# Attention projections as seven block products over two units at a time

## The chip, the core and the metric

The kernel runs on one core of one Trainium2 chip. Five engines work side by side, each through its own instructions in their order: TensorE (PE, matmuls and transposes), VectorE (DVE), ScalarE (ACT), GpSimd (POOL) and SyncE (SP, which issues every DMA of this kernel). They meet at semaphores. Operands lie in SBUF, matmuls write to PSUM, inputs, outputs and spilled tiles lie in DRAM. The metric is the device time of one execution in microseconds, lower is better.

## What is computed

The reference is a trunk of two layers over a sequence of 1024 positions and a width of 1024. Layer 0 mixes tokens with dilated sliding-window attention, layer 1 with a gated linear recurrence; each mixer is followed by a LayerNorm, a squared-ReLU MLP and another LayerNorm. The change is in the first mixer:

```python
def dilated_attention_mixer(x, w_in, w_out):
    B, S, _ = x.shape
    proj = (x @ w_in).reshape(B, S, N_GROUPS, 3, ATTN_HEADS, ATTN_HEAD_DIM)
    pos = jnp.arange(S)
    outs, lses = [], []
    for g, (window, dilation) in enumerate(DILATED_PATTERNS):
        q = rotary(proj[:, :, g, 0], pos)
        k = rotary(proj[:, :, g, 1], pos)
        o, lse = dilated_window_attention(q, k, proj[:, :, g, 2], window, dilation)
        outs.append(o)
        lses.append(lse)
    wts = jax.nn.softmax(jnp.stack(lses, axis=0), axis=0)
    o = jnp.einsum('gbsh,gbshe->bshe', wts, jnp.stack(outs, axis=0).astype(F32))
    return o.reshape(B, S, ATTN_HEADS * ATTN_HEAD_DIM).astype(x.dtype) @ w_out
```

There are 16 heads of 64, three window groups with dilations 1, 4 and 16, and so 9216 projection columns. Results are float32.

## The kernel before

To keep float32 accuracy at the faster matmul type, each operand is split into a high part (a copy rounded by ACT, L98) and a low part (raw minus high, a subtraction on DVE, L99). A product then takes three matmuls: high by high (L132), high weights by low activations (L133), low weights by high activations (L134). The helper `split` records both steps, so L98 and L99 appear for every operand in the kernel.

The unit of attention is a pair of heads in one window group: 8 pairs by 3 groups are 24 units, in the order of dilation 16, 4, 1 within a pair. A unit needs three blocks of 128 projected columns, K, Q and V. x, transposed, lies in SBUF for the whole stage as high and low parts (16 tiles). `prefetch` loads the next weight block of 512 KB and splits it whole, 128x1024. `proj` computes a block for one half of the positions: 8 k blocks by 3 matmuls of 128x512 into one of three PSUM banks ("mm"). ACT copies it out (L529 for Q and K, L533 and L536 for V, which is scattered into the order of the residue classes). When both halves of Q or K are there, `rope` sends four DMAs that swap the halves of the heads into `rot`, multiplies by the cosines on DVE (L344), by the sines on POOL (L345) and adds on DVE (L346).

The attention of a unit is cut into six steps (`pieces`): scores in pairs of blocks (L373), a mask-and-maximum on DVE (L384), exponentials on ACT (L387), transposes of the probabilities (L397, copied out by DVE for odd blocks at L401 and by ACT for even ones at L403), transposes of V (L361, copied by DVE at L362), and PV (L415). A list `fill` hangs these steps behind later half blocks: two half blocks of lag, then one step behind each. Then come `combine_tr` (maxima and sums transposed and sent through DRAM into a layout of 16 rows), `combine` (the weights of the three groups, small DVE operations, L466 to L482, then six pairs of DMAs into `frow`) and `combine_mul` (a matmul that broadcasts the weights, L497, products on DVE, L498 and L500, one addition on POOL, L499). The framework's scheduler may reorder each engine's instructions within what the data allow.

The result of each pair goes to `outproj_ln`: the first five pairs through DRAM (`SPILL`), the rest from SBUF. Its first pass accumulates seven of the eight k blocks for six of the eight row tiles, with what is left in `fill` hung in between; then come the last k block, the residual and the LayerNorm. The MLP's first matmul (L783 to L785) is already computed with seven products of blocks, with its combinations of weights on DVE (L743 to L748) and its sums out of PSUM on DVE (L796 to L818).

All large tiles come from one pool of 45 slots of 128x1024 float32. SP takes DMAs in its order, and one that waits for a slot or a producer holds up those behind it.

## Time and profile before

| what | us |
|---|---|
| median of 3 runs | 3043.63 (3040.58 to 3044.74) |
| the profiled execution | 3044.36 |
| its span, first to last instruction | 3042.6 |
| PE busy in the span | 2928.1 |
| DVE busy | 1904.1 |
| ACT busy | 1336.1 |
| POOL busy | 434.4 |

Busy time of PE is the union of its matmuls, which overlap, so a full PE is not PE at its peak. The granted TensorE clock was 0.986 of full speed over the span. In rows by group a line reads: source line, engine, operation, output from inputs, shapes, count, then busy time in all, mean of one in ns, and the idle time of the engine ahead of it with what ended it. In rows in order of time the first number is the start and the second the duration.

### The profile page before, as it was taken

The numbers are of one execution on the slowest core, as the hardware profiler recorded it, in microseconds if no ns is written. First come the engines' busy times: TensorE is split into PE (matmuls) and PEld (weight loads), VectorE is DVE, ScalarE is ACT, GpSimd is POOL, SyncE is SP. The second block draws the span as 40 slices with busy tenths as digits, with TensorE's granted clock in tenths as the row PEclk, the third lists the DMA queues.
The fourth block names the chain that finished last, engine by engine and source line by source line (L and its number), as shares of the span: only waits on it lengthen the run. The fifth ranks groups of instructions, "written<-read, shape, count | busy, mean of one in ns | idle before, by whom it ended". The sixth has DMA issues, their size and how long they took to land. (4 is left out here: it accounts for less than half of the span.)

```text
span 3042.6 us, 40183 instructions
## 1 busy us (share of the span) xinstructions
PE 2928.1 (96%) x14584; PEld 2325.6 (76%) x14584; DVE 1904.1 (63%) x3432; ACT 1336.1 (44%) x2783; POOL 434.4 (14%) x229
## 2 busy tenths in 40 slices
PE   8999999999999999899999999999999799999998
PEld 6777777777777767677778887787788677778886
DVE  5355555464554466866679786456565866679785
ACT  3343443343343441644454444455561644454442
POOL 1101011110111001200024221101010300025210
PEclk9999999999999999899999999999999899999999
DMA  4222122222222141344465653111132344465662
GB/s 143 63 57 78 44 70 64 58 71 56 60 62 61 54 146 61 124 159 152 140 241 190 212 200 116 44 56 38 54 110 71 121 163 146 141 239 195 208 231 74
DMA packets 166855, 347.78 MB, mean 114 GB/s; under 512 B 26880, under 2 KB 41344, under 8 KB 166656
## 3 DMA queue, kind: packets, MB, share of 16 engines
q1 hardware_dynamic: 166656, 345.21, 35.5%
q8 instruction: 115, 1.88, 0.3%
q14 instruction: 84, 0.69, 0.1%
HBM read 238.43 MB, written 81.13 MB: 105 GB/s over the span
## 5 line engine op out<-in xcount | busy, mean ns | idle before, releaser
L132 PE MATMUL pmm<-xh,wh 128*128 128x512 f32 x1152 | 463.9, 403 | 8.1 <-ACT wh L98 8.1
L134 PE MATMUL pmm<-xh,wl 128*128 128x512 f32 x1152 | 452.5, 393 | 1.7 <-DVE wl L99 1.7
L133 PE MATMUL pmm<-xl,wh 128*128 128x512 f32 x1152 | 453.2, 393 | 0.9 <-DVE xl L99 0.9
L387 ACT ACTIVATE p<-p,stats 128x128 f32<-128x128 f32 (+1 forms) x384 | 168.6, 441 | 227.5 <-DVE stats L384 225.2
L132 PEld LDWEIGHTS pmm<-xh,wh 128*128 128x128 f32 x1152 | 218.1, 189 | 56.7 <-ACT wh L98 8.8
L134 PEld LDWEIGHTS pmm<-xh,wl 128*128 128x128 f32 x1152 | 217.3, 189 | 49.7 <-DVE wl L99 4.0
L133 PEld LDWEIGHTS pmm<-xl,wh 128*128 128x128 f32 x1152 | 217.9, 189 | 43.4 <-DVE xl L99 1.4
L384 DVE CUSTOM_DVE_ANT_0 p<-s,mask 128x128 f32<-128x128 f32 (+1 forms) x384 | 115.5, 348 | 165.5 <-PE s L373 134.3
L345 POOL TENSOR_TENSOR rot<-rot,sinT 128x1024 f32<-128x1024 f32 x48 | 115.3, 2402 | 677.6 <-DMA rot<-e 655.7
L904 PE MATMUL pdy<-dT,dS 128*128 128x512 f32 x512 | 199.4, 389 | 0.7 <-DVE dT L99 0.7
L905 PE MATMUL pdy<-dT,dS 128*128 128x512 f32 x512 | 199.2, 389 | 0.0
L903 PE MATMUL pdy<-dT,dS 128*128 128x512 f32 x512 | 199.2, 389 | 0.0
L98 ACT ACTIVATE dS<-dr 128x512 fp32r<-128x512 f32 x192 | 120.2, 626 | 133.0 <-PE pdy L905 41.0
L99 DVE TENSOR_TENSOR dS<-dr,dS 128x512 fp32r<-128x512 f32 x192 | 165.6, 862 | 11.6 <-ACT dS L98 11.2
L99 DVE TENSOR_TENSOR wl<-wr,wh 128x1024 fp32r<-128x1024 f32 (+1 forms) x97 | 126.5, 1305 | 55.6 <-ACT wh L98 54.8
L132 PE MATMUL pmm<-f0nh,wh 128*128 128x512 f32 x384 | 153.5, 400 | 0.8 <-ACT wh L98 0.8
L133 PE MATMUL pmm<-f0nl,wh 128*128 128x512 f32 x384 | 150.0, 391 | 0.0
L134 PE MATMUL pmm<-f0nh,wl 128*128 128x512 f32 x384 | 149.9, 390 | 0.0
L529 ACT ACTIVATE e<-pmm 128x512 f32<-128x512 f32 x96 | 55.9, 590 | 207.1 <-PE pmm L134 204.6
L98 ACT ACTIVATE wh<-wr 128x1024 fp32r<-128x1024 f32 (+1 forms) x97 | 101.0, 1041 | 87.1 <-DMA wr<-in_w_attn_dram 59.0
L875 POOL TENSOR_TENSOR hold<-hold,dr 128x512 f32<-128x512 f32 x32 | 48.3, 1510 | 631.5 <-PE pup L785 599.3
L99 DVE TENSOR_TENSOR dT<-dr,dT 128x512 fp32r<-128x512 f32 x128 | 121.8, 963 | 7.5 <-ACT dT L98 6.6
(370 smaller groups left out, 6856.6 us busy)
## 6 DMA issues: line engine op xcount, KB each, us to landing
...
dr<-in_w_down_dram SPq DMA_DIRECT2D x160, 256.0 KB
...
```

The lines of the kernel that those rows point to most:

```text
L98: act(hi, raw, AF.Copy)
L99: nc.vector.tensor_sub(lo, raw, hi.bitcast(F32))
L132: nc.tensor.matmul(o, wh[:, k], xs.h(k), start=k == 0, stop=False)
L133: nc.tensor.matmul(o, wh[:, k], xs.l(k), start=False, stop=False)
L134: nc.tensor.matmul(o, wl[:, k], xs.h(k), start=False, stop=k == NK - 1)
L345: nc.gpsimd.tensor_mul(rot, rot, sinT)
L384: nc.vector.tensor_tensor_reduce(p[:, h, :n], sb[h][:, j, :n], m, -0.125, 3.0e38, op0=ALU.add, op1=ALU.min, accum_out=nm)
L387: act(p[:, h, :n], p[:, h, :n], AF.Exp, bias=sS[:, 0, h, b:b + 1], scale=-1.0, accum_out=sS[:, 1, h, b:b + 1])
L529: act(e[:, h * 512:(h + 1) * 512], o, AF.Copy)
L903: nc.tensor.matmul(o[q], h, T_[:, L], start=begin, stop=False, skip_group_check=True)
L904: nc.tensor.matmul(o[q], h, T_[:, R], start=False, stop=False, skip_group_check=True)
L905: nc.tensor.matmul(o[q], l, T_[:, L], start=False, stop=end, skip_group_check=True)
```

## The change

The projections of two consecutive units form a group; there are 12 groups. Within a group the six weight blocks form three pairs: K with Q of the first unit, K with Q of the second, V of the first with V of the second. For each pair, x (two halves of the positions by two halves of the width) and the pair of blocks are taken as 2 by 2 block matrices, and the product is made with seven block products instead of eight. A product is 4 k blocks by 3 matmuls of 128x512 (`product`). A group has 7 kinds of product by 3 pairs, 21 in all, and `seq` lists 252.

On the x side, the seven operands are made once, in the first group: four raw blocks and T1 to T4, differences of them (T1 and T2 on DVE, T3 and T4 on POOL), each split into high and low. They are written to DRAM (`keep_T`, into `xtd`), and from the second group on each operand is read back for its three products (`get_T`): the low part when the products of the operand before begin, the high part one operand earlier. On the weight side each product needs a block of 128x512 or a combination of up to four of them, which POOL computes (L407 to L419 of the new file), and a split of 128x512 on ACT and DVE (`split_w_`, five products ahead; raw blocks are loaded eight products ahead). The products' sums are taken out of PSUM by DVE additions (the new file's L655 to L670), and only the first product of a pair is copied by ACT.

The attention steps hang at fixed products of the next group (`OFFS`), about two products apart, with the two units overlapping a little. The additions that end the rotary embedding are issued two products after its DMAs. The copies of transposed V, of the odd probability blocks and of the transposed maxima move from DVE to ACT. `in_order` fixes the order of PE and of DVE to the order in which the program emits instructions, for the whole stage. `frow` becomes one tile of 12 rows, filled by six DMAs instead of twelve. The last group's two units run inside the output projection, whose first pass takes six k blocks (`NKA`) and leaves two to the second; six results go through DRAM, and the pool has 46 slots.

```diff
-NSLOT = 45
+NSLOT = 46
-SPILL = (5, 5)
+SPILL = (6, 5)
+NKA = (6, 7)
+LOADW = 8
+SPLITW = 5
+UNIT0 = 3
+KEEP = (7, 8, 10, 13, 15, 17, 20)
+OFFS = ((0, 2, 4, 7, 9, 11), (10, 12, 15, 17, 19, 21))
...
+    class in_order:
...
+        def __exit__(self, *_):
+            before = {}
+            for i in list(nc.cur_bb.bb.instructions)[self.first:]:
+                if i.engine in self.engines:
+                    if i.engine in before:
+                        tc.add_manual_dep(i, before[i.engine], mybir.DependencyInfo(
+                            mybir.DependencyClass.NoSync, mybir.DependencyReason.DATA), reason="in_order")
+                    before[i.engine] = i.name
...
-                raw = U("xraw")
-                nc.sync.dma_start(raw, xT[h, :, kk * 1024:(kk + 1) * 1024])
-                split(raw, xs[h].hi[kk], xs[h].lo[kk])
-        nc.sync.dma_start(cosT, cos_t)
-        nc.sync.dma_start(sinT, sin_t)
+        groups = [units[i:i + 2] for i in range(0, len(units), 2)]
...
+        pairs = [[(block(u, 1), block(u, 0)) for u in us] + [(block(us[0], 2), block(us[1], 2))] for us in groups]
+        ORDA = (1, 2, 6, 7, 3, 5, 4)
+        seq = [(gi, i, j) for gi in range(len(groups)) for i in ORDA for j in range(3)]
+        xtd = dp.tile([7, 2, P, 2048], F32, name="xtd")
...
+        def combine_x(name, x, y, eng):
+            xc[name] = [U("x" + name) for _ in range(2)]
+            for q in range(2):
+                eng.tensor_sub(xc[name][q], x[q], y[q])
...
+        def make_T(i):
+            v, g = nc.vector, nc.gpsimd
+            if i == 6:
+                combine_x("T1", xr["12"], xr["11"], v)
+                combine_x("T2", xr["22"], xc["T1"], v)
+            elif i == 7:
+                combine_x("T3", xr["22"], xr["12"], g)
+            elif i == 4:
+                combine_x("T4", xr["21"], xc["T2"], g)
+            src = {1: "11", 2: "21", 6: "T2", 7: "T3", 3: "22", 5: "T1", 4: "T4"}[i]
+            src = xc.pop(src) if src == "T3" or src == "T4" else xc[src] if src in xc else xr[src]
+            hi = [U("xh", F32R) for _ in range(2)]
+            lo = [U("xl", F32R) for _ in range(2)]
...
+                    split(src[q], hi[q], lo[q])
+            return hi, lo
+
+        def keep_T(m):
+            for n, part in enumerate(opT[m]):
+                for q in range(2):
+                    nc.sync.dma_start(xtd[ORDA[m] - 1, n][:, q * 1024:(q + 1) * 1024], part[q].bitcast(F32))
...
+        def get_T(m, n):
+            if m >= 7 * len(groups):
+                return
+            i = ORDA[m % 7]
+            if m < 7:
+                if m not in opT:
+                    opT[m] = make_T(i)
+                return
+            if m not in opT:
+                opT[m] = [None, None]
+            opT[m][n] = [U("xhl"[0] + "hl"[n], F32R) for _ in range(2)]
+            for q in range(2):
+                nc.sync.dma_start(opT[m][n][q].bitcast(F32), xtd[i - 1, n][:, q * 1024:(q + 1) * 1024])
...
+        def load_w(n):
+            if n >= len(seq):
+                return
+            gi, i, j = seq[n]
+            for half in {1: (0,), 2: (0,), 6: (0, 1), 7: (0, 1), 3: (0, 1), 5: (1,), 4: (1,)}[i]:
+                if (gi, j, half) not in raw:
+                    raw[gi, j, half] = U("w" + "ab"[half])
+                    nc.sync.dma_start(raw[gi, j, half], w_attn[pairs[gi][j][half]])
...
+        def split_w_(n):
+            gi, i, j = seq[n]
+            g = nc.gpsimd
+            if i in (1, 2, 4):
+                src = {1: 0, 2: 1, 4: 3}[i]
+                src = (raw[gi, j, src // 2])[:, (L, R)[src % 2]]
+            else:
+                t = U("wc")
+                c1, c2 = t[:, L], t[:, R]
+                if i == 5:
+                    g.tensor_add(c1, a21, a22)
+                    src = c1
+                elif i == 6:
+                    g.tensor_add(c1, a21, a22)
+                    g.tensor_sub(c2, c1, a11)
+                    src = c2
+                elif i == 7:
+                    g.tensor_sub(c1, a11, a21)
+                    src = c1
+                else:
+                    g.tensor_sub(c1, a11, a21)
+                    g.tensor_add(c2, c1, a12)
+                    g.tensor_sub(c1, c2, a22)
+                    src = c1
+            H[n] = parts_of(src, "H")
...
-        frow = [U("frow", F32R) for _ in range(NG)]
+        frow = U("frow", F32R)
...
-            nc.vector.tensor_mul(cls(qT, g), nat(e, g), nat(cosT, g))
-            nc.vector.tensor_add(cls(qT, g), cls(qT, g), nat(rot, g))
-            return qT
+            nc.vector.tensor_mul(cls(qT, g), nat(e, g), nat(cosT, g))
+            return qT, lambda: nc.vector.tensor_add(cls(qT, g), cls(qT, g), nat(rot, g))
-                    nc.vector.tensor_copy(vn[:, j * 512:(j + 1) * 512], pt)
+                    act(vn[:, j * 512:(j + 1) * 512], pt, AF.Copy)
-                if b % 2:
-                    nc.vector.tensor_copy(pts[:, :2 * nb * P], pt[:, :2 * nb * P])
-                else:
-                    act(pts[:, :2 * nb * P], pt[:, :2 * nb * P], AF.Copy)
+                act(pts[:, :2 * nb * P], pt[:, :2 * nb * P], AF.Copy)
-            nc.vector.tensor_copy(sr, pt[:32, 0:P])
+            act(sr, pt[:32, 0:P], AF.Copy)
+            yield
+            yield
-                    for h in range(2):
-                        r = 2 * i + h
-                        nc.sync.dma_start(
-                            frow[g][r:r + 1, :].bitcast(F32).rearrange("o (i t) -> o i t", t=P),
-                            f[8 * h:8 * h + 8, g, :].bitcast(F32))
+                    r = 4 * g + 2 * i
+                    nc.sync.dma_start(frow[r:r + 2, :].bitcast(F32).rearrange("h (i t) -> h i t", t=P),
+                                      f[:, g, :].bitcast(F32))
-                nc.tensor.matmul(fb, sel, frow[g][:, c], start=True, stop=True)
+                nc.tensor.matmul(fb, sel[:, g * P:(g + 1) * P], frow[:, c], start=True, stop=True)
...
-            og = [None] * NG
-            for g in GORD:
-                sS = small([P, 2, 2, 8], "stats", 2)
-                res = [None] * 3
-                for i, t in enumerate((1, 0, 2)):
-                    bi = ui * 3 + i
-                    prefetch(bi + 1)
-                    for h in range(2):
-                        o = proj(w, xs[h])
-                        if t < 2:
-                            act(e[:, h * 512:(h + 1) * 512], o, AF.Copy)
-                        for f in fill.pop(0) if fill else []:
-                            f()
-                        res[t] = rope(e, g, "qT" if t == 0 else "kT")
...
+        def product(n):
+            gi, i, j = seq[n]
+            o, w = bank("mm", "pmm"), H.pop(n)
+            hi, lo = opT[n // 3]
+            for k in range(4):
+                wh, wl = w[:, k * P:(k + 1) * P], w[:, 512 + k * P:512 + (k + 1) * P]
+                c = slice(k % 2 * 512, k % 2 * 512 + 512)
+                nc.tensor.matmul(o, wh, hi[k // 2][:, c], start=k == 0, stop=False)
+                nc.tensor.matmul(o, wh, lo[k // 2][:, c], start=False, stop=False)
+                nc.tensor.matmul(o, wl, hi[k // 2][:, c], start=False, stop=k == 3)
+            v = nc.vector
+            if i == 1:
+                if j != 1:
+                    p1t[0] = U("p1")
+                p1s[j] = p1t[0][:, (L, R)[j % 2]]
+                act(p1s[j], o, AF.Copy)
+                return
+            if i == 2:
+                ep[gi, j, 0] = U("vT" if j == 2 else "e")
+            if i == 6:
+                ep[gi, j, 1] = U("vT" if j == 2 else "e")
+            dx, dy = (DIL[u[1]] for u in groups[gi]) if j == 2 else (1, 1)
+            ex, ey = ep[gi, j, 0], ep.get((gi, j, 1))
+            c11, c12 = half_of(ex, 0, dx), half_of(ex, 1, dx)
+            ox, oy = (o if d == 1 else o.rearrange("p (n r) -> p n r", r=d) for d in (dx, dy))
+            px, py = (p1s[j] if d == 1 else p1s[j].rearrange("p (n r) -> p n r", r=d) for d in (dx, dy))
+            if i == 2:
+                v.tensor_add(c11, ox, px)
+                return
+            c21, c22 = half_of(ey, 0, dy), half_of(ey, 1, dy)
+            if i == 6:
+                v.tensor_add(c12, ox, px)
+                if j == 2:
+                    v.tensor_add(c21, oy, py)
+            elif i == 7:
+                v.tensor_add(c21, oy, c21 if j == 2 else c12)
+            elif i == 5:
+                v.tensor_add(c22, oy, c21)
+                v.tensor_add(c12, ox, c12)
+            else:
+                c = {3: c12, 4: c21}[i]
+                o_ = {3: ox, 4: oy}[i]
+                v.tensor_add(c, o_, c)
+
...
+            if g == GORD[-1]:
+                steps = combine(pr, ml[pr])
+                mix = [lambda: next(steps, None)] * 3
+                mix += [lambda hb=hb: combine_mul(pr, ogs[pr], hb) for hb in range(2)]
+            return [lambda: rope_of(1), lambda: rope_of(0), lambda: adds[1](), lambda: adds[0]()], [begin] + later, stats, mix
...
+        order = in_order((mybir.EngineType.PE, mybir.EngineType.DVE))
+        order.__enter__()
+        load_x("11")
+        for n in range(3):
+            load_w(n)
+        get_T(0, 0)
+        for b in ("21", "12", "22"):
+            load_x(b)
+        for n in range(LOADW):
+            load_w(n)
+        for n in range(SPLITW):
+            split_w_(n)
+        for n in range(len(seq)):
+            gi, i, j = seq[n]
+            load_w(n + LOADW)
+            if j == 0:
+                get_T(n // 3 + 1, 1)
+            if j == 1 and n // 3 >= 5:
+                get_T(n // 3 + 2, 0)
+            if n == 11:
+                constants()
+            if n == len(seq) - 1:
+                pre(oN)
+            if n == 0:
+                get_T(2, 0)
+            if n in KEEP:
+                keep_T(KEEP.index(n))
+            product(n)
+            for f in fill.pop(n, []):
+                f()
+            split_w_(n + SPLITW)
+            if n % 21 == 18:
+                last = gi == len(groups) - 1
+                base = n + 3
+                for a in range(2):
+                    ropes, core, stats, mix = unit_work(gi, a, base)
+                    if last:
+                        tail.append((ropes, core, stats, mix))
+                        continue
+                    for k, f in enumerate(ropes):
+                        at(base - 2 + 4 * a + k, f)
+                    for k, f in enumerate(core):
+                        at(base + UNIT0 + OFFS[a][k], f)
+                    e = base + UNIT0 + OFFS[a][5]
+                    at(e + 2, stats[0])
+                    for k, f in enumerate(mix):
+                        at(e + (5, 6, 7, 10, 12)[k], f)
+        order.__exit__()
+        (ra, ca, sa, _), (rb, cb, sb_, mx) = tail
+        done = [f for n in sorted(fill) for f in fill[n]]
+        lists = [[ra[0], ra[1]], [rb[0], rb[1], ra[2], ra[3]], [ca[0], rb[2], rb[3]], [ca[1]], [cb[0]]]
+        lists = [done[k:k + 1] + (lists[k] if k < len(lists) else []) for k in range(max(len(done), len(lists)))]
+        lists += [[ca[2 + k], cb[1 + k]] for k in range(4)]
+        lists += [[sa[0], cb[5]], [], [sb_[0]], [], [], [mx[0]], [mx[1]], [mx[2]], [], [], [mx[3]], [mx[4]]]
+        return oN, lists
...
+        nka = NKA[pr.mixer]
+        for k in range(NPRE, nka):
-            for ks in [range(7)] if len(tiles) == 1 else [(k,) for k in range(7)]:
+            for ks in [range(nka)] if len(tiles) == 1 else [(k,) for k in range(nka)]:
-                    rows(o, a, w, t, dm, ks, ks[0] == 0, ks[-1] == 6)
-                if len(ks) == 1 and ks[0] in (2, 4):
+                    rows(o, a, w, t, dm, ks, ks[0] == 0, ks[-1] == nka - 1)
+                if len(ks) == 1 and ks[0] in pops:
+        pops = (1, 2, 3, 4, 5, 6) if len(fill) > 12 else (2, 4)
-                pr.load_w(7)
-                pr.split_w(7, 1)
+                for k in range(nka, NK):
+                    pr.load_w(k)
+                    pr.split_w(k, 1)
-            split_k(7, h)
+            for k in range(nka, NK):
+                pr.raw[k] = oN[k]
+                split_k(k, h)
-                    rows(o, a, w, t, dm, (7,), True, True)
+                    rows(o, a, w, t, dm, range(nka, NK), True, True)
```

147 lines of the change are left out of this document (74 added, 73 removed).

## Prediction

> **What bounds the kernel now.** I read the page's totals and forty slices first, then the busy time of each engine in the attention stage and in stages after it, then the groups of that stage, then single instructions.
>
> ```profile
> span 3042.6 us, 40183 instructions
> ...
> PE   8999999999999999899999999999999799999998
> ...
> DVE  5355555464554466866679786456565866679785
> ...
> POOL 1101011110111001200024221101010300025210
> ...
> DMA  4222122222222141344465653111132344465662
> GB/s 143 63 57 78 44 70 64 58 71 56 60 62 61 54 146 61 124 159 152 140 241 190 212 200 116 44 56 38 54 110 71 121 163 146 141 239 195 208 231 74
> ```
>
> PE is full in nearly every slice; attention is about the first fourteen. There DVE stands at half, POOL at a tenth, the DMA engines at a quarter. The same by stage (columns: window, length, then busy us and count for PE, PE's weight loads, DVE, ACT, POOL; granted clock, DMA share, GB/s):
>
> ```profile
> 7.00:1095.60 1088.60, 1066.52 (x6000) 835.77 (x6001) 560.29 (x1241) 419.22 (x1107) 132.80 (x62) 1.00 0.25 70
> 1095.60:1240.00 144.40, 129.87 (x630) 98.84 (x628) 96.29 (x207) 57.52 (x138) 23.61 (x11) 0.94 0.28 99
> 0.00:20.00 20.00, 11.02 (x28) 7.37 (x29) 13.67 (x40) 11.82 (x16) 3.48 (x12) 1.00 0.90 314
> 1600.00:1700.00 100.00, 99.27 (x437) 81.52 (x436) 80.72 (x101) 46.19 (x82) 35.05 (x20) 1.00 0.55 182
> 1700.00:1800.00 100.00, 100.00 (x443) 82.81 (x442) 87.53 (x122) 50.93 (x92) 30.19 (x16) 1.00 0.69 232
> ```
>
> The first row runs from the first projection matmul to the first matmul of the output projection: 1088.6 us, PE idle for 22. So PE sets the pace. What a matmul costs there is not its duration but its distance to the next:
>
> ```profile
> L132 PE MATMUL pmm<-xh,wh 128*128 128x512 f32 x1152 | 463.9, 403 | 8.1 <-ACT wh L98 8.1
> ...
> 545.78 0.40 PE L132 MATMUL pmm<-xh,wh 128*128 128x512 f32 x1
> ...
> 549.89 0.39 PE L132 MATMUL pmm<-xh,wh 128*128 128x512 f32 x1
> ```
>
> L133 and L134 have 1152 each as well. Between the two starts lie 18 matmuls: 4.11/18 = 0.228 us, though one lasts 0.39. 3456 × 0.228 = 789 us of the 1088.6; the other 300 are scores, transposes, PV and stalls.
>
> **PE, removed.** Each group of two units needs 21 products of 12 matmuls in place of 12 half blocks of 24: 12 × 252 = 3024. 432 × 0.228 = **98.6 us less**; the floor of the stage is 990. A group then needs 21 × 2.74 = 57.5, and 300/12 = 25 for attention: 83 us. This gain counts only while PE stays the bound.
>
> **DVE.**
>
> ```profile
> L99 DVE TENSOR_TENSOR wl<-wr,wh 128x1024 fp32r<-128x1024 f32 x71 | 94.6, 1332 | 34.2 <-ACT wh L98 33.3
> L384 DVE CUSTOM_DVE_ANT_0 p<-s,mask 128x256 f32<-128x256 f32 x160 | 61.5, 421 | 61.3 <-PE s L373 35.1 <-PE ppt L397 26.1
> ...
> L346 DVE TENSOR_TENSOR kT<-kT,rot 128x1024 f32<-128x1024 f32 x24 | 44.0, 1833 | 33.0 <-POOL rot L345 30.1 <-DMA ml<-mdram 2.9
> L346 DVE TENSOR_TENSOR qT<-qT,rot 128x1024 f32<-128x1024 f32 x24 | 43.0, 1792 | 26.3 <-POOL rot L345 26.3
> L344 DVE TENSOR_TENSOR kT<-e,cosT 128x1024 f32<-128x1024 f32 x24 | 42.2, 1760 | 89.8 <-ACT e L529 89.8
> L344 DVE TENSOR_TENSOR qT<-e,cosT 128x1024 f32<-128x1024 f32 x24 | 41.9, 1748 | 12.5 <-ACT e L529 12.5
> ...
> L99 DVE TENSOR_TENSOR H<-wc,H 128x512 fp32r<-128x512 f32 x128 | 88.1, 693 | 0.6 <-ACT H L98 0.6
> L401 DVE COPY pts<-ppt 128x512 f32<-128x512 f32 (+1 forms) x96 | 57.3, 597 | 91.7 <-PE ppt L397 90.8
> L362 DVE COPY vn<-vpt 128x512 f32<-128x512 f32 x48 | 30.8, 682 | 0.0
> L796 DVE TENSOR_TENSOR upb<-pup,upa 128x512 f32<-128x512 f32 x32 | 22.1, 690 | 66.4 <-PE pup L785 66.4
> ```
>
> Gone: the block splits (95), and the copies of transposed V and probabilities (31 and 57), which move to ACT: 560 − 183 = 377. New: 252 splits of 128x512 at 0.693 (the MLP's own product splits) are 175; 22 additions out of PSUM a group, 264 at 0.690 (L796 does the same in the MLP), are 182; the scattered V additions add some 12 (half of L344's 1.76 less 0.69, 64 times); four combinations and six more splits of the activations, 10 × 1.33 = 13. Sum **759 us**, 77% of the floor.
>
> ```profile
> L98 ACT ACTIVATE wh<-wr 128x1024 fp32r<-128x1024 f32 x71 | 74.6, 1050 | 84.7 <-DMA wr<-in_w_attn_dram 57.4 <-issue 19.8 <-DMA ml<-mdram 7.5
> ...
> L529 ACT ACTIVATE e<-pmm 128x512 f32<-128x512 f32 x96 | 55.9, 590 | 207.1 <-PE pmm L134 204.6 <-issue 2.5
> ...
> L98 ACT ACTIVATE H<-wc 128x512 fp32r<-128x512 f32 x128 | 75.7, 619 | 9.8 <-DVE wc L744 9.8
> ```
>
> ACT loses 75 for block splits and 56 for evictions (more with V's), and gains 252 × 0.62 = 156 for splits, 36 × 0.59 = 21 for kept products and 88 for the copies: at most 419 + 134 = 553, half of the stage. It is not the bound.
>
> **POOL and the lock.** POOL gets 21 block combinations of 128x512 a group, 252 in all.
>
> ```profile
> L345 POOL TENSOR_TENSOR rot<-rot,sinT 128x1024 f32<-128x1024 f32 x48 | 115.3, 2402 | 677.6 <-DMA rot<-e 655.7 <-DVE mn L473 12.5 <-DVE qT L344 9.4
> ...
> L499 POOL TENSOR_TENSOR og<-og 128x512 f32<-128x512 f32 x16 | 20.4, 1272 | 369.9 <-DVE og L498 369.9
> ...
> 1643.75 6.64 POOL L884 TENSOR_TENSOR hold<-dr,hold 128x512 f32<-128x512 f32 x4 [1.97 <-ACT dS L98]
> ...
> 1645.75 1.78 DVE L885 TENSOR_TENSOR hold<-dr,hold 128x512 f32<-128x512 f32 x1
> 1647.45 1.79 DVE L99 TENSOR_TENSOR dT<-hold,dT 128x512 fp32r<-128x512 f32 x1
> ...
> 1650.86 0.68 DVE L99 TENSOR_TENSOR dS<-dr,dS 128x512 fp32r<-128x512 f32 x1
> ```
>
> Alone, such an operation takes 1.27 on POOL and 0.68 on DVE. While four ran on POOL, DVE's operations with two SBUF operands took 1.78 each, and were back at 0.68 when POOL was done: the two take turns, and a POOL operation keeps DVE out for 1.78 − 0.68 = 1.10 us. POOL's exclusive time becomes 252 × 1.10 + 48 × 2.2 (rotary) + 18 = 401 us, against 133 busy before. Splits, rotary and mixing on DVE need the lock; PSUM additions and score reductions do not.
>
> It doesn't fall evenly. Of the 21 products three (T2) need two combinations, three (T3) one, three (block 3) three, three (T1) one, nine none; so products 0 to 9 see 18 combinations prepared (five products ahead) and two rotary multiplies: 18 × 1.10 + 2 × 2.2 = 24 us. DVE's own locked work there: ten splits (6.9), six rotary operations (10.7) and some mixing (2): together **44 us**, where PE needs 27.4 + 5/12 of 25 = 38. DVE's order is fixed by the change: a split whose combination is late holds up the PSUM additions and score reductions queued behind it, and PE waits for those, since only three PSUM banks take products. PE can lead by two products and the other eleven are lighter, so part of the 6 us is recovered; I take 4 us a group for the eleven groups that carry attention, **+44**. Bounds: 0, if the lead absorbs everything (DVE at 80.7% and 87.5% with POOL at 30 to 35% left PE at 99% and more in the two rows at 1600 and 1700); and 10, if little is recovered and the waits for ACT's half of each split come on top.
>
> **DMA.** Each product group reads its operand back: 28 transfers of 512 KB a group, 14.7 MB, with 3.1 of weights and some 2.6 of rotary and spill: 20.4 MB in 83 us, 246 GB/s. At 0.90 busy 314 GB/s went through, so 349 is the limit and the load 70%; the row at 1700 has 232 at 0.69 with PE at 100%. I cost it at nothing while PE paces, covered by reads issued three and five products ahead. Uncovered, 20.4 MB at the 200 to 212 GB/s that other busy slices show would be 96 to 102 us a group. The first group is another matter: 4.2 MB of x, 9 weight blocks, 14.7 MB written, and the first read-backs queue behind them on SP: 51 transfers, 26.7 MB, 77 us, against PE at about 9 + 57.5 plus its cold start. I take 8, and 2 for the first matmul, which now waits for three 512 KB loads in place of two small ones: **+10** (bounds 3 and 20).
>
> **Tail.** Two units, not one, end inside the output projection, whose first pass shrinks to six k blocks; the mixing of the last pair is issued after its last tile.
>
> ```profile
> 1164.61 0.52 ACT L470 ACTIVATE ml<-ml 16x384 f32<-16x384 f32 x1 [12.79 <-DVE ml L469]
> ...
> 1175.18 0.39 PE L497 MATMUL fb<-frow,bsel 128*128 128x512 f32 x1
> ...
> 1185.70 0.80 PE L144 MATMUL pmm<-woh,aoh 128*128 128x512 f32 x1 [2.29 <-ACT aoh L98]
> ```
>
> From the exponential to the first broadcast lie 10.6 us, to the next projection matmul 21. Before, tiles covered all but about 6; now two tiles of 18 matmuls (8 us) stand beside it: **+8** (bounds 0 and 15). PE's attention work that moves there was counted already.
>
> **Sum.** −98.6 + 44 + 10 + 8 = −36.6 from the profiled execution's 3044.36 us (span 3042.6, the median of the runs shown 3043.63): **3008**, with 2975 to 3038 as its own range.
>
> **Rivals.** (A) PE keeps the pace and the lock waits vanish in its lead: −98.6 + 18 = −81, **2964**. For it speak the rows at 1600 and 1700; against it, that DVE there had no fixed order tied to PE's next product. (B) DVE sets the pace and the kernel is slower: DVE's 759 plus the share of POOL's 401 that hits it. From 78% on, 759 + 312 = 1071 and with 18 for start and tail the gain is gone; at 90% it is 1120 + 18 − 1088.6 = +49, **3094**. For it: the locked sum of 44 against 38, and POOL always backlogged there, so that each locked DVE operation finds it busy. Against it: eleven of 21 products have almost no POOL work. (D) A POOL operation closes DVE out for its whole 1.27 us, not for 1.10: the ten products cost 18 × 0.17 = 3 us more, eleven groups 34, **3042**; against it the row's own difference of 1.10. The Trainium skill (SBUF — State Buffer, section "SBUF: two separate sides") speaks for D: the shared ports are an exclusive lock that whichever starts first holds for the whole instruction; the trace agrees with the exclusion and differs in its length. (C) The read-backs come late: at 97 us a group, 11 × 14 more on the floor, −98.6 + 154 + 18 = +73, **3117**; against it the row with 232 GB/s at 0.69. That PE executes no fewer matmuls can be excluded from the built order.
>
> **Chances.** Forecast 0.42, A 0.27, B 0.20, C 0.06, D 0.05. A measurement of this kernel tells 0.2%, 6 us. A and nearly all of the forecast's range are faster, its end and D fall within 0.2%: faster 0.66, same 0.07, slower 0.27. The range takes in most of A and B: 2952 to 3072.
>
> **What would show it.** Projection matmuls 3024, still 0.228 apart; a group of 21 products every 87 us (83 for A, 90 and more for B). DVE busy at 90% or more of the stage with 128x512 splits well above 0.69 (under 0.9: A; 1.5: B). PE's waits on DVE, at PSUM additions, above all in products 3 to 10 of a group; waits on read-backs would mean C. If groups take 83 us and the total stays, the tail or the start was mis-sized.

## The result, and the profile after

The changed kernel takes **3117.27 us** (median of 4 runs, 3116.0 to 3118.7) beside 3042.11 for the kernel before: a ratio of **1.025, 95% interval 1.0232 to 1.0267**. The forecast of 3008 was wrong, and the range to 3072 did not hold it. First the slices of the page, to be laid beside those of before:

```profile
span 3114.2 us, 41014 instructions
...
PE   6898989799988988899999999899999899999998
...
DVE  7787687777768775976669786565565876679784
...
POOL 5654455644556510300006032110010300025200
PEclk8998999899989998999999999999999899999999
```

The first fifteen slices hold attention. DVE rose from about half to three quarters, POOL from a tenth to a half, and PE lost its nines: it is no longer the bound there. Next a table of windows, one for each group of 21 products, cut at the start of the group's first product matmul (columns as in the prediction: window, length, then busy us and count for PE, weight loads, DVE, ACT, POOL; granted clock, DMA share, GB/s; the last line sums all twelve):

```profile
8.13:97.22 89.09, 68.74 (x252) 54.15 (x253) 75.19 (x93) 29.10 (x44) 43.62 (x26) 0.87 0.74 278
...
187.26:270.68 83.42, 80.67 (x485) 63.43 (x484) 66.78 (x115) 40.17 (x115) 47.30 (x25) 1.00 0.76 232
270.68:375.17 104.49, 89.99 (x486) 69.05 (x484) 77.43 (x138) 42.13 (x117) 50.45 (x28) 0.89 0.67 205
375.17:470.02 94.85, 83.92 (x473) 64.76 (x472) 79.77 (x139) 38.98 (x116) 53.30 (x27) 0.96 0.69 210
470.02:556.36 86.34, 82.44 (x485) 64.95 (x484) 64.98 (x115) 40.49 (x115) 45.95 (x25) 0.98 0.78 236
...
sum 1123.34, PE 1000.65 PEld 776.52 DVE 864.86 ACT 467.41 POOL 590.61; mean PE 83.39 PEld 64.71 DVE 72.07 ACT 38.95 POOL 49.22
```

The groups are of three kinds, and they repeat: 104.5, 94.9, 86.3 us. The third kind has no mixing of the branches (115 operations on DVE). In the other two the three branches of a pair are mixed (23 or 24 operations more, 13 to 15 us of DVE by the rows of e4 below): in the first kind for the group's first unit, with the mixing multiplications behind products 3 and 5 (a group's products are counted from 0), in the second for its second unit, behind products 13 and 15. The stage holds three groups of each of those two and five without mixing after the first group. The five average **86.9 us, where 87 was forecast**; the other six average 100. The whole sum shows DVE busy for 77% of the stage (864.9 of 1123.3 us).

Two windows inside the 94.9 us group show how it is lost:

```profile
395.00:415.00 20.00, 15.70 (x78) 11.97 (x78) 20.00 (x28) 7.19 (x25) 19.76 (x11) 0.91 0.56 175
415.00:435.00 20.00, 14.09 (x77) 10.62 (x76) 18.19 (x40) 7.32 (x24) 13.61 (x9) 0.96 0.21 80
```

For 20 us DVE is busy without a gap and POOL beside it; PE gets 15.7 and 14.1 us of work out of 20. DVE is not full on the average (72 of 94 us), but it is full where combinations, rotary and mixing meet. The groups of DVE instructions from the second group to the end of the stage (busy us, mean ns, idle before):

```profile
L123 DVE TENSOR_TENSOR H<-wc,H 128x512 fp32r<-128x512 f32 x132 | 166.4, 1260 | 39.0 <-ACT H L122 39.0
...
L453 DVE TENSOR_TENSOR kT<-kT,rot 128x1024 f32<-128x1024 f32 x22 | 58.1, 2642 | 2.3 <-POOL rot L451 2.3
...
L453 DVE TENSOR_TENSOR qT<-qT,rot 128x1024 f32<-128x1024 f32 x22 | 50.2, 2282 | 5.6 <-POOL rot L451 5.6
...
L670 DVE TENSOR_TENSOR e<-pmm,e 128x512 f32<-128x512 f32 x44 | 30.4, 690 | 56.0 <-PE pmm L637 55.9
```

A split of a combination takes 1260 ns where 693 were counted, a rotary addition 2642 where it took 1833. The addition out of PSUM is at the 690 that was counted for it: it is not stretched.

PE's longest waits from the second group to the end of the stage (waiting instruction, what ended the wait, us in all, times, longest):

```profile
PE s L479 <- DVE stats L490: 26.2, 13, 3.1
PE mpt L544 <- DVE og L601: 24.9, 3, 8.6
...
PE pmm L635 <- DVE e L655: 6.7, 6, 1.9
```

They are for the score reductions and for a PSUM bank that a mixing multiplication frees; the PSUM additions, where the prediction looked for PE's waits, come to 6.7 us. In the first kind of group a chain is added, here in order of time (start, length, the idle time ahead and what ended it):

```profile
277.60 0.71 SPq L591 DMA_DIRECT2D frow<-fh  x1
283.99 0.62 SPq L591 DMA_DIRECT2D frow<-fl  x1
...
292.17 4.25 SPq L449 DMA_DIRECT2D rot<-e  x4
...
297.00 2.36 POOL L451 TENSOR_TENSOR rot<-rot,sinT 128x1024 f32<-128x1024 f32 x1 [4.71 <-DMA rot<-e]
299.32 1.27 POOL L602 TENSOR_TENSOR og<-og 128x512 f32<-128x512 f32 x1
...
300.63 1.77 DVE L603 TENSOR_TENSOR og<-og 128x512 f32<-128x512 f32 x1 [4.27 <-POOL og L602]
...
312.05 1.86 DVE L601 TENSOR_TENSOR og<-og,fb 128x512 f32<-128x512 f32 x3
...
312.78 0.40 PE L544 MATMUL mpt<-ident,stats 128*32 128x128 f32 x1 [7.90 <-DVE og L601]
```

SP stands for 5.7 us until the row remainder `fl` is there. Behind it in SP's queue are the rotary transfers of the other unit, so POOL waits 4.7 us for them, with the mixing addition behind that multiplication; DVE, in its fixed order, waits 4.3 us for the addition; 11 us later its next mixing multiplication frees the PSUM bank for which PE has stood 7.9 us.

### The profile page after: what moved, and what is told of

It is laid out like the page before. It is cut to its first block, busy times and chain, and to the rows that moved or that the text cites. A ratio compares the mean times of both kernels' runs of the same rounds, so it can differ in the third digit from the quotient of the medians.

```text
span 3114.2 us, 41014 instructions
## 1 busy us (share of the span) xinstructions
PE 2881.6 (93%) x14152; PEld 2276.1 (73%) x14152; DVE 2237.5 (72%) x3717; ACT 1402.3 (45%) x3028; POOL 906.3 (29%) x483
## 4 chain that ended last, share of the span: by engine, by line
PE 44%; DMA 6%; DVE 5%; ACT 2%; issue 1%; POOL 1%; SPq 0%; DVEq 0%; ACTq 0%; POOLq 0%
PE pup L988 5%; PE pup L990 5%; PE pup L989 5%; PE pdy L1109 4%; PE pdy L1108 4%; PE pdy L1110 4%; PE pmm L156 3%; DMA wb<-in_w_up_dram 3%; PE pmm L157 3%; PE pmm L158 3%; PE pdx L1110 2%; PE pdx L1109 2%; PE pdx L1108 2%; DMA d<-hd 1%; PE ho L1369 1%
## 5 line engine op out<-in xcount | busy, mean ns | idle before, releaser
L635 PE MATMUL pmm<-xh,H 128*128 128x512 f32 x1008 | 421.6, 418 | 41.4 <-ACT H L122 14.3
L636 PE MATMUL pmm<-xl,H 128*128 128x512 f32 x1008 | 407.1, 404 | 5.9 <-DMA xl<-xtd 5.9
L637 PE MATMUL pmm<-xh,H 128*128 128x512 f32 x1008 | 405.9, 403 | 0.0
L123 DVE TENSOR_TENSOR H<-wc,H 128x512 fp32r<-128x512 f32 x272 | 266.9, 984 | 45.5 <-ACT H L122 45.3
L635 PEld LDWEIGHTS pmm<-xh,H 128*128 128x128 f32 x1008 | 199.9, 198 | 88.7 <-ACT H L122 25.5
L451 POOL TENSOR_TENSOR rot<-rot,sinT 128x1024 f32<-128x1024 f32 x48 | 133.3, 2779 | 401.5 <-DMA rot<-e 318.4
L122 ACT ACTIVATE H<-wc 128x512 fp32r<-128x512 f32 x272 | 165.2, 623 | 183.7 <-POOL wc L414 69.7
L636 PEld LDWEIGHTS pmm<-xl,H 128*128 128x128 f32 x1008 | 198.6, 197 | 45.2 <-DMA xl<-xtd 6.6
L637 PEld LDWEIGHTS pmm<-xh,H 128*128 128x128 f32 x1008 | 197.1, 196 | 44.6 <-DVE H L123 0.5
L122 ACT ACTIVATE dS<-dr 128x512 fp32r<-128x512 f32 x192 | 120.1, 626 | 122.0 <-DVE dT L123 43.3
L199 POOL TENSOR_TENSOR z<-z,bB 128x1024 f32<-128x1024 f32 x24 | 60.1, 2507 | 273.5 <-ACT z L198 270.6
L123 DVE TENSOR_TENSOR H<-wa,H 128x512 fp32r<-128x512 f32 x136 | 108.6, 800 | 24.1 <-ACT H L122 24.1
```

What stands on the lines that cost most here:

```text
L122: act(hi, raw, AF.Copy)
L123: nc.vector.tensor_sub(lo, raw, hi.bitcast(F32))
L635: nc.tensor.matmul(o, wh, hi[k // 2][:, c], start=k == 0, stop=False)
L636: nc.tensor.matmul(o, wh, lo[k // 2][:, c], start=False, stop=False)
L637: nc.tensor.matmul(o, wl, hi[k // 2][:, c], start=False, stop=k == 3)
```

## The experiments

The group times below are means from the start of one group's first product to the next's, taken as in the table of windows. "None" are the five groups without mixing, "1st" and "2nd" the three each that mix for their first and second unit (three, where some expectations speak of four: the fourth pair of that kind is mixed behind the stage). "Stage" is the start of the output projection.

| kernel | us | ratio to before, 95% | first group | none | 1st | 2nd | stage |
|---|---|---|---|---|---|---|---|
| changed | 3117.27 | 1.0232–1.0267 | 89.1 | 86.9 | 104.8 | 95.1 | 1131.5 |
| e1 combinations on DVE | 3153.03 | 1.0349–1.0380 | 87.9 | 91.3 | 102.8 | 101.3 | 1164.7 |
| e2 multiplications later | 3108.07 | 1.0205–1.0235 | 88.8 | 87.8 | 99.6 | 95.3 | 1120.5 |
| e3 no read-backs | 3076.41 | 1.0101–1.0131 | 89.0 | 87.7 | 97.6 | 87.5 | 1091.1 |
| e4 no combinations | 3020.99 | 0.9920–0.9954 | 70.9 | 80.9 | 101.6 | 82.3 | 1035.3 |
| e5 mixing addition on DVE | 3114.50 | 1.0230–1.0267 | 88.4 | 87.4 | 103.7 | 95.4 | 1131.1 |
| e6 72 combinations shared | 3100.31 | 1.0174–1.0212 | 80.2 | 88.6 | 105.0 | 90.9 | 1119.0 |
| e7 no fixed order | 3127.99 | 1.0266–1.0300 | 88.8 | 93.3 | 98.9 | 99.1 | 1157.2 |
| e9 rows later too | 3121.01 | 1.0247–1.0282 | 89.3 | 87.8 | 97.7 | 95.4 | 1116.0 |
| e10 e9 and e6 | 3092.11 | 1.0155–1.0189 | 80.6 | 87.8 | 95.8 | 90.4 | 1086.4 |
| e11 e9 and e4 | 2997.18 | 0.9847–0.9876 | 70.7 | 81.0 | 87.2 | 82.8 | 993.9 |
| e12 e10, 36 on DVE | 3094.59 | 1.0164–1.0195 | 80.6 | 88.5 | 96.0 | 90.4 | 1090.5 |
| e13 combinations not waited for | 3110.18 | 1.0204–1.0241 | 86.1 | 87.3 | 103.8 | 96.0 | 1129.9 |
| e14 rotary on ACT's queue | 3153.99 | 1.0347–1.0383 | 89.4 | 90.5 | 105.9 | 97.8 | 1160.9 |
| e15 e10, tail and slots | 3081.14 | 1.0106–1.0141 | 80.1 | 88.5 | 96.5 | 91.2 | 1094.0 |
| e16 no mixing | 3001.60 | 0.9854–0.9883 | 89.0 | 87.0 | 86.4 | 85.0 | 1046.4 |
| e17 read-backs behind rotary | 3132.83 | 1.0282–1.0316 | 89.2 | 88.1 | 107.6 | 95.1 | 1145.9 |
| e18 four sums, rows later | 3058.18 | 1.0039–1.0072 | 77.3 | 87.9 | 92.9 | 89.4 | 1072.3 |

### What POOL's combinations cost: e4, e13, e1

Code cuts show the lines that matter; "..." stands for more edits of the same run.

```diff
 e4: all combinations gone
...
+                src = a22 if i == 5 else a21 if i == 6 else a11 if i == 7 else a12
```

> The 252 block combinations are left out: each product takes a raw block as its weights, so the outputs are not the projection's; number of products, splits, transfers and mixing stay. It is the upper bound of what POOL's new work costs. Theory POOL (lock and queue together): splits back to 0.69 us, rotary additions back to 1.8, groups of 83 to 87 us, total 3000 to 3035. Rival DMA: total within 10 us of 3117. Rival mixing by its own latency (transfers of the rows and DVE's chain, not POOL): groups with mixing still 8 us or more over those without, total 3060 to 3085.

96 us less. Windows of groups of the three kinds, and the sum over all twelve:

```profile
242.32:345.12 102.80, 87.55 (x486) 67.34 (x484) 68.11 (x138) 41.56 (x117) 12.40 (x6) 0.92 0.69 207
345.12:427.39 82.27, 81.06 (x473) 62.54 (x472) 66.23 (x139) 38.44 (x116) 12.38 (x6) 1.00 0.74 243
427.39:507.18 79.79, 79.79 (x486) 63.09 (x484) 52.69 (x115) 40.26 (x115) 11.88 (x4) 1.00 0.77 254
...
sum 1027.11, PE 964.97 PEld 752.22 DVE 728.87 ACT 461.63 POOL 146.10; mean PE 80.41 PEld 62.69 DVE 60.74 ACT 38.47 POOL 12.18
```

Without combinations PE is full in the third kind (79.79 of 79.79, so the floor of a group is 80, not 83), and the second kind's mixing costs 1.4 us in place of 8.2 (82.3 − 80.9, 95.1 − 86.9). The first kind keeps its 102: that part is not POOL's combinations, and the mixing rival was right for it. Of the 96.2 us of the stage's sum, 60.5 are PE's idle time (122.7 to 62.1) and 35.7 are PE's busy time, for the same matmuls.

The starts of the products in the traces say where the groups without mixing lose. In those at 187, 470 and 757 us of the changed kernel products 0 to 9 take 40.3, 43.2 and 42.8 us, in e4 36.6 to 37.5; the other eleven take 43.2 in both. So the loss lies in the ten products in which the prediction saw it. But it does not fall with the number of combinations prepared there: e6 has 15 of them in place of 18 and takes 43.4 to 44.7 us, e18 has 12 and takes 43.3 to 44.7. Why these ten take some 43 us with any of the three numbers is **open**.

```diff
 e13: combinations computed, splits take raw blocks
-                    src = c2
+                    src = a21
```

(and likewise for the other three kinds of product.)

> The 252 block combinations are computed on POOL as in the changed kernel, but no split waits for them: each product splits a raw block instead (so the outputs are not the projection's). POOL's work, its lock and its queue ahead of the rotary multiplications stay; only the way from a late combination to the splits and products is cut. The kernel without combinations took 3021, the changed one 3117. Theory lock (POOL's operations stretch DVE's): locked splits still 0.9 us or more, total 3090 to 3117. Theory late combination (splits and all behind them on DVE wait for POOL): total 3021 to 3050. Both in part: between.

Only 7 us come back. A group of the second kind, and the largest group of splits on DVE:

```profile
376.70:471.93 95.23, 86.09 (x473) 65.88 (x472) 82.06 (x139) 38.23 (x116) 53.51 (x27) 0.95 0.68 209
```

```profile
L123 DVE TENSOR_TENSOR H<-wa,H 128x512 fp32r<-128x512 f32 x128 | 136.8, 1069 | 35.0 <-ACT H L122 35.0
```

Splits of raw blocks, which wait for no combination, take 1069 ns: they are stretched without the late combination, and waiting for it carries only 7 of the 96 us. What e13 leaves in is the lock and POOL's queue ahead of the rotary multiplications, for which DVE waited 7.9 us in the changed kernel (2.3 and 5.6 in the rows above); no run takes these two apart, so that the lock carries most of the rest is argued from that small wait.

```diff
 e1
-            g = nc.gpsimd
+            g = nc.vector
```

> The 252 block combinations of the weights run on DVE in place of POOL; everything else as in the changed kernel. It adds 252 x 0.69 = 174 us of work to DVE and takes away POOL's queue ahead of the rotary and mixing operations and most of the lock. Theory POOL (combinations on POOL stretch DVE's locked operations by some 155 us in the stage and keep rotary and mixing operations waiting in POOL's queue): the groups with mixing at products 3 and 5 come down from 104.5 us to 90 to 95, the total to 3060 to 3090. Rival DVE (its own work is already the pace): another 174 us of DVE work cannot be hidden, groups of 95 us and more everywhere, total 3117 to 3180. Rival DMA (read-backs late): same within 6 us, since the transfers do not change.

36 us slower, the DVE rival's case. Most of the lock is gone (the splits of combinations average 729 ns), but DVE has the additions itself:

```profile
L123 DVE TENSOR_TENSOR H<-wc,H 128x512 fp32r<-128x512 f32 x132 | 96.3, 729 | 97.3 <-ACT H L122 95.9 <-DMA xh<-xtd 1.4
```

On DVE the combinations cost 132 us (3153.03 − 3020.99), on POOL 96. So moving them to POOL saves about a quarter of their cost. That DVE's time is what counts, whether it goes into work or into the lock, fits both runs.

### Why the groups with mixing: e16, e2, e5, e9, e11, e7

```diff
 e16: combine() returns at once; in combine_mul
-            for g in GORD:
+            for g in ():
-            nc.gpsimd.tensor_add(og[2][:, c], og[2][:, c], og[1][:, c])
-            nc.vector.tensor_add(acc[:, c], acc[:, c], og[2][:, c])
```

> The mixing of the three attention branches is left out (its small operations, rows, broadcasts, multiplications and additions; the first branch alone goes on, so the output is not the reference's); combinations, read-backs, rotary, score statistics and spill stay. In the changed kernel the groups without mixing took 83 to 90 us, those with it 95 and 105. Theory mixing on top of the lock (13 to 15 us of DVE work fall into the stretch where DVE is already full): all eleven groups come to 84 to 90, the stage is 60 to 80 us shorter, and with the wait of 9.6 us at the end of the tail the total is 3020 to 3050. Rival POOL alone (mixing groups are long because of rotary and combinations that fall together there): second-unit groups still 92 or more, total 3070 to 3100.

116 us less, more than expected. The groups that had taken 104.5 and 94.9 us:

```profile
276.01:362.83 86.82, 83.07 (x479) 64.63 (x478) 66.78 (x118) 41.36 (x116) 47.97 (x26) 0.98 0.79 247
362.83:448.53 85.70, 81.89 (x467) 63.82 (x466) 67.43 (x118) 38.19 (x114) 50.24 (x26) 0.96 0.77 242
```

All eleven average 86.3 with every combination, read-back and lock in place, and the splits of combinations are stretched even more than before (from the second group to the end of the stage):

```profile
L123 DVE TENSOR_TENSOR H<-wc,H 128x512 fp32r<-128x512 f32 x132 | 187.9, 1423 | 37.0 <-ACT H L122 37.0
```

85 us come in the stage and 27 in the output projection's part. The starts of the products place the loss. In the first kind 13.2 to 15.5 us pass from the start of product 3 to the next and 14.6 to 15.2 from that of product 5, the two with mixing multiplications; in e16 it is 5.1 to 6.2 and 6.5 to 6.6, but in e4, without combinations, 10.4 to 11.5 and 15.2 to 17.9. In the second kind products 11 to 13 take 19.6 to 20.0 us together, 11.3 to 11.4 in e16 and 12.8 to 12.9 in e4. So the second unit's mixing costs its 8.2 us only beside the combinations, while the first unit's costs 17.9 beside them (104.8 − 86.9) and 20.7 without (101.6 − 80.9): its place and its chain cost the time, also where DVE has room.

```diff
 e2: the first unit's multiplications behind products 10 and 12
-at(e + (5, 6, 7, 10, 12)[k], f)
+at(e + ((5, 6, 7, 17, 19), (5, 6, 7, 10, 12))[a][k], f)
```

> The two mixing multiplications of the first unit of a group are issued behind products 10 and 12 in place of 3 and 5; nothing else is moved, no work added or taken away. Theory mixing (the PSUM bank of a broadcast is freed by a multiplication on DVE that stands in the stretch where POOL has most combinations, and PE waits for it in its fixed order): the four groups of 104.5 us come down to some 95, those of 95 stay, total 3075 to 3090. Theory lock alone (DVE is stretched in the first ten products of every group, mixing or not): the same locked time, total within 10 us of 3117. Rival DMA: same within 6 us.

Of the 9 us asked of the first kind 5 came; 3108 is outside what the mixing theory expected, and just within the 10 us that the theory of the lock alone allowed.

```diff
 e5
-            nc.gpsimd.tensor_add(og[2][:, c], og[2][:, c], og[1][:, c])
+            nc.vector.tensor_add(og[2][:, c], og[2][:, c], og[1][:, c])
```

> The 16 additions of the mixing, 128x512, move from POOL to DVE, at the same place in the program; combinations, transfers and everything else as in the changed kernel. DVE gets 16 x 0.69 = 11 us more. Theory queue (the addition stands behind a rotary multiplication and combinations in POOL's queue, and DVE, in its fixed order, waits for it with all score reductions, splits and PSUM additions behind it): DVE's wait for POOL in the mixing goes (8.4 us in one place of the kernel without combinations, 4.3 in the changed kernel), the four groups of 104.5 us come down to 95 to 99, those of 95 by 1 to 3; total 3085 to 3100. Rival transfers (PE waits for the mixing's rows, not for the addition): groups of 102 to 105, total 3110 to 3125.

Nothing. The addition went, but POOL still stood for the rotary transfer, with the next combinations behind it:

```profile
301.82 2.40 POOL L451 TENSOR_TENSOR rot<-rot,sinT 128x1024 f32<-128x1024 f32 x1 [13.12 <-DMA rot<-e]
```

The addition is one passenger of the queue, not its cause.

```diff
 e9: as e2, and the rows' transfers four products later
...
             v.tensor_sub(fl, l, fh.bitcast(F32))
+            yield
```

> As the run with the mixing multiplications behind products 10 and 12, and besides the six small transfers of the mixing rows are issued four products later, behind the eight rotary transfers of the other unit; in the groups where the mixing belongs to the second unit they move by one product. No work is added or taken away. In that earlier run SP stood from 280.2 to 285.9 for the row remainder fl, and the rotary transfers behind it came so late that POOL waited 4.3 us for them with combinations queued behind. Theory SP queue (the rows' issue holds up SP, and with it the rotary transfers, POOL's queue, the splits and PE): the groups of 99.5 us come down to 90 to 94, total 3075 to 3090. Rival POOL backlog (the combinations alone set those groups): 98 to 100 us, total within 6 us of 3108.

> The rows' transfers and mixing multiplications later, and the 252 block combinations left out (raw blocks as weights, so the outputs are not the projection's). In the kernel without combinations the four groups with the first unit's mixing still took 101 to 103 us, the others 80 to 82. Theory SP queue: those come down to 80 to 86, total 2940 to 2965. Rival latency of the mixing itself: 95 or more, total 3000 to 3021.

With combinations the first kind comes from 99.6 to 97.7, a miss; the SP queue alone is worth 2 us beside them. Without combinations it comes from 101.6 to 87.2:

```profile
242.71:331.21 88.50, 84.74 (x485) 65.31 (x484) 66.24 (x138) 42.11 (x117) 16.66 (x7) 0.98 0.78 241
331.21:413.50 82.29, 81.05 (x473) 62.51 (x472) 64.91 (x139) 38.39 (x116) 12.25 (x6) 1.00 0.73 239
```

So place and queue together are worth 14 us a group of the first kind without combinations (101.6 − 87.2) and 7 beside them (104.8 − 97.7). Both kernels lost 18 to 22 us behind the stage, where PE waited 21.2 us in each for a rotary result; which of the shifted steps caused that was not tried by itself.

```diff
 e7
-        order.__enter__()
-        order.__exit__()
```

> The fixed order of PE and DVE over the attention stage is left off, so that the scheduler places their instructions as it does elsewhere; no work is added or taken away. Theory order (a late addition or combination costs so much because everything behind it on DVE and PE must wait): the groups with mixing come down, total 3060 to 3105. Rival work (POOL's lock and queue set the time whatever the order): 3110 to 3130. It can be worse, 3130 to 3200, if the scheduler's own order puts products ahead of what frees their banks.

Groups of the first kind get 6 us shorter and the other two kinds 4 to 6 longer: on the whole the fixed order is not what costs the time.

### The read-backs: e3, e14, e17

```diff
 e3
-            if m not in opT:
-                opT[m] = [None, None]
+            opT[m] = opT[6]
+            return
```

> From the second group on, every product uses the operand tiles of the last product of the first group, which stay in SBUF: the 308 read-back transfers of 512 KB (161 MB) are left out, so what is computed there is not the projection; matmuls, splits, combinations and mixing are as many as before. Theory DMA (read-backs late, the 3117 of the prediction's rival C): groups of 83 to 88 us, total 3030 to 3050. Theory POOL and mixing: only the waits that show a transfer at their end go (5.9 us for a read-back at 111.7, up to 20 us for the small transfers of the mixing rows and the rotary halves, which share the queues), total 3090 to 3112, groups with mixing still over 98 us.

41 us less, though the changed kernel shows one wait of 5.9 us for a read-back. Both theories missed. The groups, from the first kind:

```profile
271.62:368.79 97.17, 87.01 (x486) 67.21 (x484) 76.12 (x132) 40.68 (x116) 51.30 (x30) 0.93 0.26 67
368.79:456.10 87.31, 81.86 (x473) 63.63 (x472) 80.18 (x138) 39.45 (x116) 50.58 (x27) 0.98 0.24 68
456.10:543.32 87.22, 82.66 (x485) 64.94 (x484) 67.27 (x120) 40.10 (x115) 48.39 (x25) 0.96 0.20 56
```

Again the groups without mixing do not move (86.9 and 87.7), and those with it get 7 to 8 us shorter, with DVE as busy as before. The read-backs' price, too, is paid only in the groups with mixing: from the start of product 3 to the next it is 5.8 to 6.4 us in the first kind (13.2 to 15.5 before), and products 11 to 13 take 12.3 in the second (19.6 to 20.0 before).

```diff
 e14
-                nc.sync.dma_start(rot[b4 * 32:b4 * 32 + 32, :], e[o:o + 32, :])
+                nc.scalar.dma_start(rot[b4 * 32:b4 * 32 + 32, :], e[o:o + 32, :])
 e17: get_T from the second group on moved behind the steps of its product
```

> The 192 rotary transfers are issued by ACT in place of SP; nothing else is moved. They no longer stand on SP behind the mixing's rows and the read-backs, but the read-backs still take the 16 DMA engines beside them. Leaving out the read-backs had given 41 us. Theory issue queue (the 41 us come from the rotary transfers' place behind them on SP): groups with mixing 3 to 8 us shorter, total 3080 to 3105. Rival engines (the 16 DMA engines are shared, whoever issues) or ACT's own loss (192 issues of 0.6 us, 118 us, in front of its casts): 3117 or more, to 3160.

> The read-backs of the second group on are issued behind the rotary transfers and the mixing's transfers of the same product, in place of ahead of them; nothing else. Theory place (the 41 us that the read-backs cost come from their standing ahead of the rotary transfers on SP by one product): groups with mixing 3 to 8 us shorter, total 3085 to 3105. Rival bandwidth and queue as such (some 20 MB a group pass the same queue and engines, wherever one product's issue stands): within 8 us of 3117; later reads may also be waited for, to 3130.

Both are slower, and neither settles it. e14 loses in every kind of group, which ACT's issues explain only by argument. In e17 one product's later issue is enough to make the read-backs late themselves, 5.9 us of waits becoming 29.9:

```profile
PE pmm L636 <- DMA xl<-xtd: 29.9, 4, 7.7
```

**Open** is whether the 41 us go through SP's order, through the shared DMA engines, through the moment at which POOL's burst begins, or through the slots that the read-back tiles take, which e3 leaves free as well.

### The slots: e8

```diff
-NSLOT = 45
+NSLOT = 46
```

> The kernel before with 46 in place of 45 slots in the pool of working tiles; nothing else. The stages behind attention take some 12 us longer in the changed kernel, although only the slot count and the placement of tiles touch them (and one more unit's spill). Theory slots (the other placement in the pool makes the MLP stages slower): 3047 to 3056. Rival spill and tail (what the attention stage leaves behind is later or larger): same as before, 3038 to 3046.

The kernel before with 46 slots takes 3049.03 beside 3041.14: 1.0025, interval 1.0014 to 1.0036: 8 us for the slot count on the kernel before. From the MLP's first matmul to the end the kernels with 45 slots take 1812.4 us (before) and 1812.0 (e15), those with 46 take 1819.3 (e8), 1824.4 (changed) and 1822.9 (e10), so the extra slot costs the changed kernel about as much or a little more. One place where it shows is the down projection of the first MLP, here in before, in before with 46, in the changed kernel, and in e15, which has 45 again:

```profile
1619.00:1884.80 265.80, 261.85 (x1160) 213.13 (x1158) 211.39 (x328) 126.77 (x249) 66.66 (x33) 0.99 0.51 169
```

```profile
1615.50:1886.10 270.60, 262.39 (x1159) 213.11 (x1157) 210.98 (x328) 126.30 (x249) 70.35 (x33) 0.99 0.49 162
```

```profile
1680.20:1952.00 271.80, 263.04 (x1159) 212.97 (x1157) 211.56 (x328) 126.02 (x249) 69.85 (x34) 0.99 0.50 162
```

```profile
1658.00:1923.40 265.40, 260.90 (x1160) 212.06 (x1158) 210.70 (x328) 126.62 (x249) 65.56 (x33) 1.00 0.52 169
```

### Towards a better version: e6, e10, e12, e15, e18

```diff
 e6: T1 takes the kept sum of T2, block 3 the kept difference of T3
-                    g.tensor_add(c1, a21, a22)
-                    src = c1
+                    src = wcs.pop((gi, j, 6))[:, L]
...
-                    g.tensor_sub(c1, a11, a21)
 e12: beside e10, the difference of T3 on DVE
-                    g.tensor_sub(c1, a11, a21)
+                    nc.vector.tensor_sub(c1, a11, a21)
 e15: beside e10, with the last pair's mixing steps at their old places
-NSLOT = 46
+NSLOT = 45
...
 e18: beside rows later, block 3 from the kept sum of T2
-                    g.tensor_sub(c1, a11, a21)
-                    g.tensor_add(c2, c1, a12)
-                    g.tensor_sub(c1, c2, a22)
+                    g.tensor_sub(c1, a12, wcs[gi, j][:, R])
...
```

> The sum a21+a22 of the T2 product is kept for the T1 product, and the difference a11-a21 of the T3 product for the block-3 product, so POOL has 180 combinations in place of 252; results unchanged, no other work moved. Theory POOL (the 252 combinations cost 96 us, as the kernel without them showed, in proportion): 72/252 x 96 = 27 us less, total 3085 to 3095. Rival burst (only those of T2, six a group at one place, hurt; the ones taken away here belong to the T1 and block-3 products): under 10 us, 3107 to 3117. Rival DMA: same within 6 us.

> The rows' transfers and mixing multiplications later, and the 72 shared combinations, together. The shared ones alone gave 17 us. Both theories of POOL and of SP's queue add: 3117 - 17 - (28 to 42), total 3055 to 3075. If the two act on the same wait, no better than the better one of them alone.

> As the run with the rows later and shared combinations, and the 36 differences a11-a21 of the T3 product on DVE in place of POOL: POOL is left with 144 combinations, DVE gets 36 x 0.69 = 25 us. Theory POOL: 36 fewer combinations are worth 0.38 us each of the time (96/252), 14 us, less what DVE's 25 us cost where it is the later engine (the kernel with all 252 on DVE lost 36 us): between 10 us faster and 5 us slower than the run without this edit. Rival DVE: slower by 10 us or more.

> Three edits that gave something, together: 180 combinations in place of 252, the mixing rows' transfers and multiplications later (except for the last pair before the tail, which keeps its place, since moving it cost the tail 18 us), and 45 slots, which the kernel before has. The run with the first two took 3092; less 18 for the tail and 8 for the slots: 3060 to 3075. It does not reach the 3042 of the kernel before, as long as no group with mixing comes under 90 us. If the slot pool of 45 holds up the read-backs: 3075 to 3095.

> Two edits: the block-3 product takes its weights as a12 less the kept sum a21+a22-a11 of the T2 product, and the T1 product the kept sum a21+a22, so that POOL has four combinations for each set of three blocks' products in place of seven, 144 in all in place of 252, results unchanged; and the mixing rows and multiplications of the first unit come later, as in the run that did so, but not for the last pair before the tail, whose steps keep their places. By the parts: 108 fewer combinations, of which 72 fewer were worth 17, some 25 us; the later rows 15 us in the stage (1131.5 to 1116.0) without the 18 that the tail lost; 3117 - 25 - 15 = 3077, 3065 to 3090. Theory lock: the groups without mixing come to 82 to 86, those of the second unit to 87 to 90. Rival (the mixing alone decides, combinations are no longer what counts): under 10 us from the combinations, 3090 to 3105. The 3042 of the kernel before is not reached by either.

e6 gives 17 us, less than in proportion (27); 9 of them in the first group. e10 has 15 us of e9's loss behind the stage and ends at 3092, not at the 3055 to 3075 expected. e12 is 2.5 us slower, which the two sets of runs (3086.07 to 3093.69 and 3089.9 to 3100.39) do not tell apart: these 36 operations gain nothing by moving from POOL to DVE. e15 misses its 3060 to 3075: its tail was not mended (174.3 us to the MLP's first matmul, where the changed kernel takes 158.3). Its 3081 lies in the 3075 to 3095 named for slots that hold up the read-backs, and the rows bear that out in part: SP stood 103.3 us in all with read-backs behind POOL's combinations for block 3, 52.8 in e10, and the stage ends 7.6 us later. e18 does more than expected, 59 us under the changed kernel, by 108 combinations fewer and the later rows together, with the last pair's steps left alone; the two edits were not run apart:

```profile
262.06:354.77 92.71, 86.45 (x486) 66.59 (x484) 75.26 (x138) 42.13 (x117) 37.80 (x19) 0.96 0.75 229
354.77:443.99 89.22, 83.22 (x473) 64.05 (x472) 76.69 (x139) 38.70 (x116) 39.04 (x18) 0.98 0.71 221
```

Against the lock theory's number, the groups without mixing did not come under 86 (87.9). e18 is still 0.56% slower than the kernel before; none of the versions that compute the whole beats it.

## Why the prediction was wrong, step by step

- **PE's gain** was right: 3024 projection matmuls, and a group of 79.8 to 81 us when nothing else is in the way (e4), against 83.
- **DVE's own work, ACT:** the prices held (0.690 for additions out of PSUM; ACT 467 us in the stage, at most 553 said).
- **POOL and the lock, the step that failed:** "and some mixing (2)" in the sum of 44 us for the ten heavy products, spread over all groups alike, and with it "+44". The mixing is 13 to 15 us of DVE in six of eleven groups, and the transfers and waits that it puts ahead of PE had no term. Three groups take 17.9 and three 8.2 us more than those without it, together **78 us**, and e16 shows that the mixing brings them: without it all eleven take 86.3. In the second kind it costs so much only beside the combinations; in the first its place and chain cost as much without them (20.7 in e4). Without mixing the number holds, 87 forecast and 86.9 measured, but in part by luck: PE's floor is 2 us lower than said and the wait 6 us in place of 4, and by the sum's own price (1.10 us for each combination) e18 should have saved 6.6 us in the ten products, and saved none. The prediction's "DVE busy at 90% or more of the stage" did not come: it was 77%, and a stretch of 20 us at 100% was enough.
- **The moved steps on SP:** the rows' transfers ahead of the rotary ones were not costed at all. e11 against e4 shows 14 us a group of the first kind for their place and the multiplications' together.
- **DMA at nothing while PE paces:** PE did not pace, and e3 gives 41 us. Rival C had the right total, 3117, by a mechanism that the rows don't show: groups of 97 everywhere, from reads waited for. The 41 overlap with the 78 (they come in the same six groups) and are not added to them; by what way they cost stays open.
- **Start, +10:** the first group took 89.1 us in place of 67.5, **22 us** missed, and not by DMA as said: without combinations it takes 70.9, with them on DVE 87.9. The transfers' share was about right; the first combinations had no price in the sum.
- **Tail, +8:** the output projection's part grew from 134.6 to 158.3 us, of which 12.5 are the attention of one more unit: 11, near enough.
- **Not in the sum:** the slot count, 8 us on the kernel before and some 11 between e10 and e15 behind the MLP's first matmul.

So 109 us were missed: 78 in the groups with mixing, 22 in the first, and 9 behind the stage, to which the slots belong. Rival B, with DVE as the pace at 3094, was the nearest in kind, though it too spread the loss over all groups; A, that PE's lead absorbs the lock, is refuted by the windows at 395 and 415. D's 1.10 or 1.27 us can't be told apart in these sums.
